# Second-layer single experts: fp32 matmuls straight from the weight slots in place of high and low parts

## The chip, the cores and the metric

The kernel runs on one core of a Trainium2 chip. The metric is the device time of one execution in microseconds; the profile is one execution taken apart by the hardware profiler. TensorE (PE in the profile, its weight loads PEld) multiplies, VectorE (DVE), ScalarE (ACT) and GpSimd (POOL) do the elementwise work, SyncE's queue (SP, SPq) issues nearly all weight transfers, and the core's 16 DMA engines carry them.

## The reference

Two layers over 256 latent and 256 context tokens of width 1024. The first has Fourier mixing and a short convolution, the second pooling and windowed attention; the change touches neither. After the mixer each layer has a mixture of 16 experts with top-2 routing. In the second layer only the 256 latent tokens pass through it:

```python
for e in range(N_EXPERTS):
    hid = jax.nn.silu(h @ w_gate[e]) * (h @ w_up[e])
    out = out + combine[:, e:e + 1] * (hid @ w_down[e])
```

An expert's gate and up are 1024 x 512 and its down is 512 x 1024, all fp32, 2 MB each: 6 MB an expert, 96 MB for the layer. All of it is read once from HBM.

## The kernel before

**Units.** The experts are ranked by load on the chip and dealt into units of 128 token slots: a single (`S`) has one expert for 128 slots, a pair (`P`) two experts with 64 each, a quad (`Q`) four with 32 each. For the second layer `PLAN[1] = "PPSPSPPQ"`, so eight units, numbered 0 to 7 here: pairs 0, 1, 3, 5, 6, singles 2 and 4, and the quad 7 at the end.

**A unit's work on TensorE.** `xpose1` makes the gathered tokens' transpose `xh`; `gu` does gate and up (8 steps over k each, into a 128 x 512 bank, by `mm_unit`, L933), `hidden` takes silu(gate) x up x weight, `hid_T` transposes that, `down1` does the 8 down matmuls (`mm_down`, L967), `combine1` brings the result back to token order (L1708) and adds it to H. In the loop (L1727 on) the order is: down of the unit before, up of this one, combine of the one before, transposes and gate of the next. A pair's or quad's experts use plain fp32 operands, in disjoint column groups of the array, side by side. A single's matmul is three products of fp32r parts (`mm3`, L517 to L519): high x high, high x low, low x high.

**Parts.** For a single, `Stream._prep` makes the parts of each weight load in two pieces: ScalarE writes the high part `whi` (L176), VectorE or, for each third piece, GpSimd the low part `wlo` (L180). The ring holds `NPIECE` = 4 pieces, which is two loads. The tokens and the hidden rows of singles are split as well (`split`, and `hl` in `hid_T`). Earlier stages of the kernel, the second layer's mixer last among them, use the same ring of parts.

**The stream of weights.** Every weight load is 1 MB and has a place in one list (`st.add`), in the order of use: for each unit its gate loads, then the down loads of the unit before, then its up loads. A pair has 4 loads for each matrix, a single 2, the quad 8. A load starts when a slot of 1 MB is free:

```python
def load(self):
    while self.free and self.loaded < min(len(self.src), self.limit):
        ...
        self.owner[i] = self.free.pop(0)
def _prep(self):
    ...
            if j == 1:
                self._release(i)
```

A slot of a pair or quad is free again when TensorE has read it (`done`), that of a single once both of its pieces are split (`_prep`, above), which comes right after its load in the program's order. All loads are issued by SP in one queue, so one that waits for its slot holds back those behind it. In the second layer there are 13 slots: 7 in the ring, one in `fp`, four in the phase's own pool (`EXTRA`), and one made of two 512 KB tiles (class `Two`: tiles `wa` and `wb`), which takes its load as two transfers (L140; a whole one is L147).

The order of instructions on each engine is set by the framework's planner, from the program's order and its own timeline.

Of the kernel before, what the change touches and what calls it, by code (L numbers as in the profile page):

```python
# [10 lines left out]
F32 = mybir.dt.float32  # L11
F32R = mybir.dt.float32r
# [6 lines left out]
KD = 8  # L19
# [9 lines left out]
RING, NPIECE = 7, 4  # L29
# [183 lines left out]
def backbone(ctx: ExitStack, tc: tile.TileContext, I, out):  # L213
    nc = tc.nc
    V, S, G, T, Q = nc.vector, nc.scalar, nc.gpsimd, nc.tensor, nc.sync

    cp = ctx.enter_context(tc.tile_pool(name="cp", bufs=1))
    ring = ctx.enter_context(tc.tile_pool(name="ring", bufs=1))
# [14 lines left out]
    def tr_t():  # L233
        return psum.tile([128, 512], F32, name="tr", tag="tr", bufs=2)


    st = Stream(tc, ring, RING, NPIECE)
# [59 lines left out]
    def expert(l, p):  # L297
        if p < FIXED[l]:
            return slice(p, p + 1)
        if (l, p) not in which:  # L300
            which[l, p] = nc.values_load(ids[l][0:1, p:p + 1], engines=[mybir.EngineType.SP], min_val=0,
                                         max_val=NE - 1)
        return ds(which[l, p], 1)

    def add_moe(l):
        def src(w, p, r0, c0):
            return [(lambda t: t, lambda: w[expert(l, p), r0:r0 + 512, c0:c0 + 512].rearrange(
                "a (k p) f -> (a p) k f", p=128))]

        def flat(t):  # L310
            return t.rearrange("p k f -> p (k f)")

        def rows_of(w, p, s):

            return [(flat, lambda: w[expert(l, p)].rearrange("a (p s j) f -> s (a p) (j f)", p=128, s=2)[s])]

        def put(name, w, u, pos, last=False):
            for s, (r0, c0) in enumerate(pos):
                for p in u:
                    st.add((name, l, p), src(w, p, r0, c0) if l == 0 or last else rows_of(w, p, s), len(u) == 1)  # L320

        wg, wu, wd = (I[n][l] for n in ("moe_w_gate", "moe_w_up", "moe_w_down"))
        rows2, cols2 = ((0, 0), (512, 0)), ((0, 0), (0, 512))
        for n, u in enumerate(UNITS[l]):
            put("g", wg, u, rows2)
            if n:
                put("d", wd, UNITS[l][n - 1], cols2)
            put("u", wu, u, rows2)
        put("d", wd, UNITS[l][-1], cols2, True)
# [186 lines left out]
    def mm3(o, lh, ll, rh, rl, first, last):  # L516
        T.matmul(o, lh, rh, start=first, stop=False)  # L517
        T.matmul(o, lh, rl, start=False, stop=False)  # L518
        T.matmul(o, ll, rh, start=False, stop=last)  # L519

    def split(hi, lo, x, eng):
        i = S.activation(hi, x, AF.Copy)  # L522
        eng.tensor_sub(lo, x, hi.bitcast(F32))  # L523
        return i
# [117 lines left out]
    with phase("even") as ep:  # L642
        def big(name, tag, dt=F32):
            return ep.tile([128, KD, 512], dt, name=name, tag=tag)
# [15 lines left out]
        xT = big("xT", "XT")  # L660
# [199 lines left out]
        r0 = []  # L860
# [20 lines left out]
        for half in range(2):  # L881
            banks = [mm_t() for _ in range(4)]
            hs = slice(half * 512, half * 512 + 512)
            for s in range(2):
                adas(4 + half * 2 + s)
                w = st.take(("eo", half))
# [33 lines left out]
    def mm_unit(o, l, n, name, xh, xl, s, first, last, between=()):  # L920

        u = UNITS[l][n]
        w = [st.take((name, l, p)) for p in u]
        i = st.taken - len(u)
        for k in range(4):
            kk = s * 4 + k
            if len(u) == 1:
                mm3(o, xh[:, kk], xl[:, kk], w[0].h(k), w[0].l(k), first and k == 0, last and k == 3)
            else:
                m = 128 // len(u)  # L930
                for h in range(len(u)):
                    hs = slice(h * m, h * m + m)
                    T.matmul(o[hs], xh[:, kk, hs].bitcast(F32), w[h][:, k], start=first and k == 0, stop=last and k == 3,  # L933
                             skip_group_check=True)
            if k == 1 and len(u) == 1:
                st.half()
            if k == 3:
                for h in range(len(u)):
                    st.done(i + h)
            if k % 2:  # L940
                for f in between[k // 2:k // 2 + 1]:
                    f()
# [11 lines left out]
    def mm_down(os, l, n, hh, hl, s):  # L954

        u = UNITS[l][n]
        w = [st.take(("d", l, p)) for p in u]
        i = st.taken - len(u)
        for k in range(4):
            j, o = 2 * s + k // 2, os[k % 2]  # L960
            if len(u) == 1:
                mm3(o, hh[:, j], hl[:, j], w[0].h(k), w[0].l(k), j == 0, j == 3)
            else:
                m = 128 // len(u)
                for h in range(len(u)):
                    hs = slice(h * m, h * m + m)
                    T.matmul(o[hs], hh[:, j, hs].bitcast(F32), w[h][:, k], start=j == 0, stop=j == 3,  # L967
                             skip_group_check=True)
            if k == 1 and len(u) == 1:
                st.half()  # L970
            if k == 3:
                for h in range(len(u)):
                    st.done(i + h)
# [82 lines left out]
    def hid_T(pool, hid, pair, rows=False):  # L1056
        pt = tr_t()
        for q in range(4):

            T.transpose(pt[:, q * 128:(q + 1) * 128], hid[:, q:512:4] if rows else hid[:, q * 128:(q + 1) * 128], idt)  # L1060
        hh = pool.tile([128, 4, 128], F32R, name="hh", tag="hh", bufs=1)
        if pair:
            V.tensor_copy(hh.bitcast(F32).rearrange("p k t -> p (k t)"), pt)
            return hh, None
        hl = pool.tile([128, 4, 128], F32R, name="hl", tag="hl", bufs=1)
        p4 = pt.rearrange("p (k t) -> p k t", k=4)
        S.activation(hh, p4, AF.Copy)  # L1067
        V.tensor_sub(hl, p4, hh.bitcast(F32))
        return hh, hl
# [64 lines left out]
    with phase("moe0") as mp:  # L1134
        xT = {}
# [26 lines left out]
        units = UNITS[0]  # L1162
# [126 lines left out]
        for n in range(NU):  # L1289
# [12 lines left out]
            hid = hidden(mp, pg, pu, slw[:, n:n + 1])  # L1302
# [26 lines left out]
        for c in range(2):  # L1329
            t = ("whi", "wlo")[c]  # L1330
# [19 lines left out]
    with phase("odd") as op:  # L1350
# [90 lines left out]
        w = st.take(("okv",), 256)  # L1441
# [15 lines left out]
        for b in range(2):  # L1457
            pt = tr_t()
# [6 lines left out]
        pt = tr_t()  # L1465
# [75 lines left out]
        units = [(b, c) for b in range(2) for c in range(4)]  # L1541
# [15 lines left out]
        fs = []  # L1557
# [16 lines left out]
        for n, u in enumerate(units):  # L1574
# [9 lines left out]
            if n == 4:  # L1584
                flush()
                rows(1, 3, 5, 1)
                t = op.tile([128, 2, D], F32, name="s4b", tag="band")
# [4 lines left out]
            if n in (4, 5):  # L1592
                w = st.take(("oo", n - 4))
# [26 lines left out]
    with phase("moe1") as mp:  # L1620
        for n in range(EXTRA):
            st.more(1, lambda n=n: mp.tile([128, 4, 512], F32, name="w", tag=f"w{n}"))
        st.load()
        m5b = mp.tile([128, D], F32, name="m5b1")
        spread(m5b, 1, 5, 0)
        units = UNITS[1]
        NU = len(units)
        ranks, ranksT = pm, None
        xT, slw, sgT, xg = {}, {}, {}, {}
# [38 lines left out]
        def xpose1(n, sg=None):  # L1668

            xh = mp.tile([128, KD, 128], F32R, name="xh1", tag="xh", bufs=2)  # L1670
            xl = mp.tile([128, KD, 128], F32R, name="xl1", tag="xl", bufs=1) if len(units[n]) == 1 else None
            for hf in range(2):
                pt = tr_t()
                for q in range(4):

                    ks = slice(hf * 4 + q, D, 8)
                    o = pt[:, q * 128:(q + 1) * 128]
                    if sg is None:
                        T.transpose(o, xg[n][:, ks], idt)
                    else:  # L1680
                        for c in range(2):
                            T.matmul(o, f1[c][:, ks], sg[:, c], start=(c == 0), stop=(c == 1))
                fs = slice(hf * 4, hf * 4 + 4)
                if xl is None:
                    (V.tensor_copy if hf else S.copy)(xh[:, fs].bitcast(F32).rearrange("p k t -> p (k t)"), pt)
                else:
                    split(xh[:, fs], xl[:, fs], pt.rearrange("p (k t) -> p k t", k=4), V)
            xT[n] = (xh, xl)

        def slotsT1(n):  # L1690
            pb, io = spread_ranks(units[n], ranksT, 256)
# [6 lines left out]
        def down1(n, hh, hl):  # L1698
            ys[n] = [x_t(f"{t}1", "Y", F32R) for t in ("yh", "yl")]
            down(mp, 1, n, hh, hl, *ys[n])  # L1700
# [25 lines left out]
        reg = any_over(mp, over)  # L1726
        for n in range(NU):  # L1727
            if n:
                down1(n - 1, *hid_T(mp, hid, len(units[n - 1]) > 1, True))
            pu = gu("u", 1, n, *xT[n])  # L1730
            hid = hidden(mp, pg, pu, slw[n])
            slotsT1(n)
            if n:
                combine1(n - 1)
            if n + 1 < NU:
                xpose1(n + 1)
                if n + 3 < NU:
                    slots1(n + 3)
                    gather1(n + 3)
                pg = gu("g", 1, n + 1, *xT[n + 1])  # L1740

        hh, hl = hid_T(mp, hid, len(units[-1]) > 1)
        gfb = mp.tile([128, D], F32, name="gfb", tag="xl", bufs=1)
        Q.dma_start(gfb, I["final_g"].partition_broadcast(128))
        yb = x_t("yb", "Y")
# [119 lines left out]
```

## Time and profile before

| | us |
|---|---|
| three runs | 1009.97 median, 1009.04 to 1010.44 |
| the profiled execution, its own time | 1012.91 |
| its span, first to last instruction | 1011.1 |
| granted clock, mean over the span | 0.958 of full speed |

The second layer's experts fill the last quarter. Their first matmul is at 751.5 us of the span; the phase's own loads begin at 737.9. In the stretches below, PEclk 1.00 is the 2.4 GHz level and 0.50 the 1.2 GHz one. A timeline row has start, length, engine, line, operation, tiles and the number of records merged; behind it in brackets the idle time before it and what ended it. A plain fp32 matmul leaves two records.

### The profile page before, as it was taken

The page shows a single profiled execution, that of the slowest core. Times are in us where ns is not written, and L with a number is a line of the kernel's source. Part 1 is how long each engine was busy: PE and PEld are TensorE (multiplying, and loading weights), DVE is VectorE, ACT ScalarE, POOL GpSimd, SP SyncE. Part 2 cuts the span into 40 slices and gives each one's busy share as a digit, 9 for nine tenths or more (in the row PEclk, how much of TensorE's full clock was granted, in tenths as well). Part 3 has the DMA queues.
Part 4 walks back from the last instruction along what each step waited for, and adds up shares of the span by engine and source line. Part 5 has one row for each costly group of instructions (what it writes and reads, how often), then busy time and mean ns, then how long its engine had stood idle before and what let it go on. Part 6 is the DMA issues. An engine that isn't in the chain of part 4 may idle for free. (4 is left out here: it accounts for less than half of the span.)

```text
span 1011.1 us, 12687 instructions
## 1 busy us (share of the span) xinstructions
PE 927.9 (92%) x4662; PEld 583.7 (58%) x4662; DVE 532.2 (53%) x921; ACT 340.3 (34%) x488; POOL 346.5 (34%) x239
## 2 busy tenths in 40 slices
PE   4999999978899999999999788999976999999973
PEld 2677677746675678558746567457553355544321
DVE  4552525286783777457935774547443265643212
ACT  4322113144563266246534362333211132411001
POOL 3350103335562746525823633023000143452112
PEclk9999999998899999999999989799977999999988
DMA  9973668948699799799699872296568799999993
GB/s 316 363 266 125 230 252 290 352 167 299 214 321 374 245 344 362 264 340 387 219 363 385 292 237 84 94 308 237 191 232 326 293 418 407 370 384 419 420 397 132
DMA packets 116276, 296.28 MB, mean 293 GB/s; under 512 B 6632, under 2 KB 16888, under 8 KB 105704
## 3 DMA queue, kind: packets, MB, share of 16 engines
q1 hardware_dynamic: 110184, 278.06, 75.0%
q0 software_dynamic: 5984, 17.26, 4.7%
q8 instruction: 40, 0.66, 0.3%
q14 instruction: 36, 0.29, 0.1%
q10 hardware_dynamic: 32, 0.01, 0.0%
HBM read 295.45 MB, written 4.24 MB: 296 GB/s over the span
## 5 line engine op out<-in xcount | busy, mean ns | idle before, releaser
L176 ACT ACTIVATE whi<-w 128x1024 fp32r<-128x1024 f32 x182 | 190.7, 1058 | 221.9 <-PE mm L519 87.0
L180 POOL TENSOR_TENSOR wlo<-w,whi 128x1024 fp32r<-128x1024 f32 x64 | 164.6, 2572 | 258.8 <-ACT whi L176 206.0
L180 DVE TENSOR_TENSOR wlo<-w,whi 128x1024 fp32r<-128x1024 f32 x118 | 181.1, 1546 | 92.5 <-ACT whi L176 91.8
L933 PE MATMUL mm<-w,xh 128*64 128x512 f32 (+1 forms) x616 | 150.9, 617 | 4.8 <-DMA w<-in_moe_w_up_dram 4.8
L528 POOL TENSOR_TENSOR H<-H,am 128x512 f32<-128x512 f32 x64 | 89.7, 1420 | 125.3 <-DVE am L527 122.9
L933 PEld LDWEIGHTS mm<-w,xh 128*64 128x64 f32 (+1 forms) x616 | 43.8, 135 | 88.4 <-issue 78.1
L517 PE MATMUL mm<-whi,xh 128*128 128x512 f32 x192 | 79.3, 413 | 1.9 <-DVE am L527 1.1
L518 PE MATMUL mm<-wlo,xh 128*128 128x512 f32 x192 | 78.6, 409 | 2.7 <-DVE wlo L180 2.3
L519 PE MATMUL mm<-whi,xl 128*128 128x512 f32 x192 | 78.1, 407 | 0.0
L527 DVE TENSOR_TENSOR am<-mm,m5b 128x512 f32<-128x512 f32 x64 | 42.9, 684 | 28.7 <-PE mm L1261 19.5
L1261 PE MATMUL mm<-y,seT 128*128 128x512 f32 x208 | 54.5, 397 | 0.2 <-ACT y L522 0.2
L517 PE MATMUL mm<-aTh,whi 128*128 128x512 f32 x128 | 52.4, 415 | 1.0 <-ACT aTh L678 1.0
L518 PE MATMUL mm<-aTl,whi 128*128 128x512 f32 x128 | 51.6, 403 | 1.1 <-POOL aTl L679 1.1
L519 PE MATMUL mm<-aTh,wlo 128*128 128x512 f32 x128 | 51.1, 400 | 0.0
L1261 PEld LDWEIGHTS mm<-y,seT 128*128 128x128 f32 x208 | 38.1, 188 | 15.5 <-issue 4.9
L518 PEld LDWEIGHTS mm<-wlo,xh 128*128 128x128 f32 x192 | 37.4, 195 | 14.4 <-DVE wlo L180 3.4
L517 PEld LDWEIGHTS mm<-whi,xh 128*128 128x128 f32 x192 | 37.5, 195 | 14.0 <-issue 4.2
L445 PE MATMUL yp<-w,sT 128*32 128x512 f32 x288 | 44.0, 624 | 0.0
L519 PEld LDWEIGHTS mm<-whi,xl 128*128 128x128 f32 x192 | 37.4, 195 | 7.7 <-DVE xl L523 0.3
L517 PE MATMUL yp<-whi,hh 128*128 128x512 f32 x96 | 38.2, 397 | 0.7 <-ACT hh L1067 0.7
L1053 DVE SCALAR_TENSOR_TENSOR sg<-sg,slw,mm 128x512 f32<-128x512 f32 x21 | 15.6, 742 | 43.9 <-PE mm L933 41.1
L518 PE MATMUL yp<-wlo,hh 128*128 128x512 f32 x96 | 38.4, 400 | 0.0
(363 smaller groups left out, 1545.2 us busy)
## 6 DMA issues: line engine op xcount, KB each, us to landing
w<-in_moe_w_gate_dram SPq DMA_DIRECT2D x60, 1024.0 KB, 11.3
w<-in_moe_w_down_dram SPq DMA_DIRECT2D x59, 1024.0 KB, 10.5
w<-in_moe_w_up_dram SPq DMA_DIRECT2D x57, 1024.0 KB, 9.7
w<-in_ada_w_dram SPq DMA_DIRECT2D x48, 1024.0 KB, 10.1
w<-in_even_w_in_dram SPq DMA_DIRECT2D x8, 1024.0 KB, 9.6
w<-in_odd_w_in_dram SPq DMA_DIRECT2D x5, 1024.0 KB, 14.3
w<-in_even_w_out_dram SPq DMA_DIRECT2D x4, 1024.0 KB, 7.9
s4b<-mrow SPq DMA_DIRECT2D x6, 512.0 KB
```

What stands on the lines that cost most here:

```text
L176: self.nc.scalar.activation(hi, t, AF.Copy)
L180: eng.tensor_sub(lo, t, hi.bitcast(F32))
L445: T.matmul(pa[32 * j:32 * j + 32, :], s_at(s * 4 + j, u), t[:, j, :], start=first and s == 0, stop=last and s == 1, skip_group_check=True)
L517: T.matmul(o, lh, rh, start=first, stop=False)
L518: T.matmul(o, lh, rl, start=False, stop=False)
L519: T.matmul(o, ll, rh, start=False, stop=last)
L527: V.tensor_mul(t, pp, m)
L528: eng.tensor_add(acc, acc, t)
L933: T.matmul(o[hs], xh[:, kk, hs].bitcast(F32), w[h][:, k], start=first and k == 0, stop=last and k == 3, skip_group_check=True)
L1053: V.scalar_tensor_tensor(sg, sg, w, pu, op0=OP.mult, op1=OP.mult)
L1261: marks["comb"] = T.matmul(pp, seT[n][:, c * 128:(c + 1) * 128], t[:, hs], start=(i == 0), stop=(i == 2 * len(ns) - 1))
```

## The change

The second layer's singles are no longer split. `put` marks none of that layer's loads as split, and `mm_unit` and `mm_down` choose the three products by whether a low part was passed instead of by the unit's size. `xpose1` copies the tokens without a low part, `hid_T` is called as for pairs. A single's matmuls thus run as plain fp32 over all 128 columns, on weights in their slots, and its slots are freed by TensorE. The memory of the ring's four high and four low pieces becomes four more slots, each a `Two` of one `whi` and one `wlo`, added behind the four `EXTRA` ones: 17 in all.

```diff
         def put(name, w, u, pos, last=False):
...
-                    st.add((name, l, p), src(w, p, r0, c0) if l == 0 or last else rows_of(w, p, s), len(u) == 1)
+                    st.add((name, l, p), src(w, p, r0, c0) if l == 0 or last else rows_of(w, p, s),
+                           l == 0 and len(u) == 1)
...
-            if len(u) == 1:
+            if xl is not None:
                 mm3(o, xh[:, kk], xl[:, kk], w[0].h(k), w[0].l(k), first and k == 0, last and k == 3)
...
-            if k == 1 and len(u) == 1:
+            if k == 1 and xl is not None:
                 st.half()
...
-            if len(u) == 1:
+            if hl is not None:
                 mm3(o, hh[:, j], hl[:, j], w[0].h(k), w[0].l(k), j == 0, j == 3)
...
         for n in range(EXTRA):
             st.more(1, lambda n=n: mp.tile([128, 4, 512], F32, name="w", tag=f"w{n}"))
+
+        for n in range(NPIECE):
+            st.more(1, lambda: Two(*(ring.tile([128, 1024], F32R, name="w2", tag=t, bufs=NPIECE).bitcast(F32)
+                                     for t in ("whi", "wlo"))))
         st.load()
...
-            xl = mp.tile([128, KD, 128], F32R, name="xl1", tag="xl", bufs=1) if len(units[n]) == 1 else None
...
-                if xl is None:
-                    (V.tensor_copy if hf else S.copy)(xh[:, fs].bitcast(F32).rearrange("p k t -> p (k t)"), pt)
-                else:
-                    split(xh[:, fs], xl[:, fs], pt.rearrange("p (k t) -> p k t", k=4), V)
-            xT[n] = (xh, xl)
+                (V.tensor_copy if hf else S.copy)(xh[:, fs].bitcast(F32).rearrange("p k t -> p (k t)"), pt)
+            xT[n] = (xh, None)
...
-                down1(n - 1, *hid_T(mp, hid, len(units[n - 1]) > 1, True))
+                down1(n - 1, *hid_T(mp, hid, True, True))
...
-        hh, hl = hid_T(mp, hid, len(units[-1]) > 1)
+        hh, hl = hid_T(mp, hid, True)
```

## Rows read from the trace of the kernel before

**Rows 1.** The page's first part: busy time and share of each engine.
```profile
PE 927.9 (92%) x4662; PEld 583.7 (58%) x4662; DVE 532.2 (53%) x921; ACT 340.3 (34%) x488; POOL 346.5 (34%) x239
```

**Rows 2.** Windows: busy us of each engine, then PEclk, DMA share, GB/s.
```profile
752.00:796.00 44.00, 35.79 (x157) 14.50 (x155) 15.18 (x53) 6.96 (x8) 5.52 (x4) 0.84 0.66 251
796.00:856.00 60.00, 57.70 (x262) 29.32 (x259) 30.08 (x46) 14.64 (x19) 19.12 (x13) 0.97 1.02 421
856.00:868.00 12.00, 10.67 (x50) 7.96 (x49) 9.93 (x15) 6.85 (x10) 5.61 (x4) 1.00 0.81 292
...
896.00:904.00 8.00, 8.00 (x31) 3.51 (x31) 1.17 (x2) 0.60 (x2) 3.01 (x2) 1.00 0.87 304
904.00:964.00 60.00, 59.84 (x311) 24.90 (x314) 17.11 (x26) 6.04 (x11) 13.40 (x11) 1.00 1.01 420
964.00:994.00 30.00, 19.53 (x90) 4.52 (x87) 3.50 (x5) 1.45 (x4) 4.03 (x4) 0.89 0.96 361
```

**Rows 3.** TensorE's timeline in the quad's up and down, 961 to 998 us.
```profile
961.19 3.91 PE L933 MATMUL mm<-w,xh 128*32 128x512 f32 x32
...
971.54 1.07 PE L933 MATMUL mm<-w,xh 128*32 128x512 f32 x3 [2.74 <-DMA w<-in_moe_w_up_dram]
...
978.89 0.66 PE L1060 MATMUL tr<-idt,sg 128*128 128x128 f32 x4 [0.84 <-DVE sg L1053]
...
980.33 1.06 PE L933 MATMUL yp<-w,hh 128*32 128x512 f32 x6 [0.78 <-DVE hh L1063]
...
988.36 1.04 PE L933 MATMUL yp<-w,hh 128*32 128x512 f32 x2 [2.17 <-SPq L1130]
...
989.34 1.98 PE L1763 MATMUL mm<-yb,sgT 128*128 128x512 f32 x4
...
993.63 3.62 PE L933 MATMUL yp<-w,hh 128*32 128x512 f32 x26 [1.33 <-SPq L1130]
```

**Rows 4.** SP's waits from 690 us on: total, times, longest.
```profile
SPq L147 <- PE mm L933: 62.4, 25, 14.4
SPq L147 <- DVE wlo L180: 56.5, 11, 11.9
```

**Rows 5.** SP's timeline: issues of weight loads in the second layer's experts.
```profile
737.94 2.14 SPq L147 DMA_DIRECT2D w<-in_moe_w_gate_dram  x4
...
755.17 6.63 SPq L147 DMA_DIRECT2D w<-in_moe_w_down_dram  x3
...
768.19 15.46 SPq L147 DMA_DIRECT2D w<-in_moe_w_gate_dram  x2
793.14 2.05 SPq L147 DMA_DIRECT2D w<-in_moe_w_down_dram  x4
...
956.56 25.02 SPq L147 DMA_DIRECT2D w<-in_moe_w_down_dram  x8
```

**Rows 6.** TensorE's timeline: pairs' gates, a single's first and last product, two waits.
```profile
783.31 11.10 PE L933 MATMUL mm<-w,xh 128*64 128x512 f32 x42
...
811.13 0.47 PE L517 MATMUL mm<-whi,xh 128*128 128x512 f32 x1
...
816.54 0.40 PE L519 MATMUL mm<-whi,xl 128*128 128x512 f32 x1
...
820.43 0.80 PE L518 MATMUL mm<-wlo,xh 128*128 128x512 f32 x1 [2.29 <-DVE wlo L180]
...
863.76 0.47 PE L517 MATMUL mm<-whi,xh 128*128 128x512 f32 x1 [1.11 <-DVE am L527]
...
888.25 7.09 PE L933 MATMUL mm<-w,xh 128*64 128x512 f32 x32
```

**Rows 7.** A window of 4 us behind the first of those waits.
```profile
820.00:824.00 4.00, 3.56 (x8) 2.12 (x10) 3.27 (x5) 2.12 (x2) 0.00 (x0) 0.57 1.04 429
```

**Rows 8.** DMA issues from 740 us on: the token gathers, median us to landing.
```profile
xg<-fd,sli POOLq DMA_INDIRECT x7, 7.2
```

**Rows 9.** SP's timeline: the first half of a load into the slot of two tiles.
```profile
802.85 0.34 SPq L140 DMA_DIRECT2D wa<-in_moe_w_up_dram  x1
```

More of the change, by code (lines that the diff above doesn't have):

```diff
@@ L968, in mm_down @@
                              skip_group_check=True)
-            if k == 1 and len(u) == 1:
+            if k == 1 and hl is not None:
                 st.half()
```

## The prediction

> **What bounds the kernel now.** I read the page first. TensorE is busy for 92% of the span [rows 1], which speaks against a change that gives it more to do. An average over stages doesn't settle that, so the second layer's experts come next, in windows [rows 2]. From 752 to 796 us the DMA engines move 251 GB/s, from 796 to 856 they are full at 421, twice they fall back (292 and 304), and from 904 on they are full again. TensorE is busy all the while, with under 3 us idle from 796 to 856 and next to none from 904 to 964. Only in the last stretch, 964 to 994, is it idle for a third of the time, with the DMA engines still loaded. The timeline there [rows 3] names the wait: the quad's up waits 2.74 us for a load of up weights, the second half of its down 2.17 and 1.33 us for loads (SPq stands there for a DMA that came last). The last load lands at about 993.6, and the last down matmul ends at 993.63 + 3.62 = 997.25; from there to the end of the span are 13.9 us which the change doesn't touch.
>
> So the end is set by the last weight load. TensorE outruns the transfers from 796 on, lives on what is stored in the slots, and finds them empty at 964. What would bring the last load forward is transfer time not used earlier. Measured against 421 GB/s, 752 to 796 loses 44 x (1 - 251/421) = 17.8 us, 856 to 868 loses 12 x (1 - 292/421) = 3.7, 896 to 904 loses 8 x (1 - 304/421) = 2.2: together 23.7 us. SP's waits say why [rows 4]: 62.4 us for slots that TensorE still reads, 56.5 us for slots whose low part isn't made. The first case of the second kind is in SP's timeline [rows 5]. The two gate loads of unit 2, the first single, take from 768.19 to 783.65, and the next issue is at 793.14: in the program's order the second goes into the slot that the first one's split frees, and unit 1's down load into the slot that the second one's frees. SP can't pass them.
>
> **The change, part by part.**
>
> *Products.* A single has 16 gate and up steps and 8 down steps; two singles make 48. Now a step is three products: from the first to the last of 24 in a gate are 816.54 - 811.13 = 5.41 us, 0.235 each, 0.706 a step [rows 6]. After it is one plain fp32 matmul of 128 columns, two records. The pair's gate gives the spacing: 32 records in two column groups in 7.09 us, (7.09 - 0.59)/15 = 0.433 a record, 0.866 a matmul. That shape at full width stands once in the trace, four records in 1.98 us [rows 3], the first one's start and the last one's tail included, so 0.99 is an upper bound. I take 0.866, since the singles' matmuls come in rows of eight as the pair's do: 48 x (0.866 - 0.706) = 7.7 us more, at most 13.6.
>
> The Trainium skill speaks against the change here: its page FP8 and Floating Point Precision, section TensorE Precision Notes, has true fp32 as four passes through the array. If one product is one pass, a step costs 4 x 0.235 = 0.94 us and the sum is 11.2 us instead of 7.7; the trace's two records in 0.866 us lie between three and four of its own products.
>
> *Splits.* Gone are 24 pieces on ScalarE, 16 on VectorE and 8 on GpSimd, and the two halves of the tokens' and hidden rows' splits. None of these engines sets the end, so they count only where TensorE waited: 2.29 us for a low part at 820.43 and 1.11 us for a bank that VectorE was late to read at 863.76 [rows 6]. Behind the first the granted clock over 4 us is 0.57 of full [rows 7]; the eight records there stand at 0.235/0.57 = 0.41 us and cost 1.4 us more. Together 4.8 us less. TensorE's net is +2.9 us, with 0 and +13.6 as bounds (0 if the planner's new order closes some of the small gaps between the blocks too).
>
> *Slots.* The list's order for the first units is gate 0, up 0, gate 1, down 0, up 1, gate 2, down 1, up 2, gate 3. Thirteen slots hold it to the first load of down 0. After, the four new slots take all of down 0, and their memory is free when the mixer's last product has read the parts, ahead of the routing and so of these loads. With gate and up 0 read by 768 [rows 5], the old kernel has issued 21 loads and the chained 22nd goes at 783.65; the new one has issued 25. One load is 1.049 MB, 2.49 us at 421 GB/s. From 739.7 on the new kernel has 16 loads (gate 1, down 0 and the eight after them), half a MB of the modulation row and two gathers of half a MB: about 17.5 x 2.49 = 43.6 us, to 783.3. Then all is full until TensorE is half through gate 1 and gives back two slots, as now: 42 records from 783.31 take 11.10 us [rows 6], the 16th ends near 788; first bytes flow at 789. That leaves 5.5 us idle of the 17.8, so 12.3 us are won by 796. The two later losses, behind splits of the singles' loads too, are worth 5.9 us more. The last load lands 12.3 to 18.2 us earlier, at 981.3 to 975.4.
>
> At the end 17 slots hold the quad's eight up and eight down loads together. Now the eight down issues stretch over 25.02 us [rows 5], since they wait for up slots; after, they follow the release of unit 6's down slots, which lies ahead of the quad's up at 961.19 [rows 3].
>
> *What a single's slot now costs.* It is free only after TensorE's use instead of after the split, so of the four new slots two make good for the four pieces, which held two loads. It shows where TensorE is at a single: 6.9 us for two slots, in which 2.8 loads arrive. I take 1 to 3 us of idle transfers there, within the two ends above.
>
> *DMA work moved.* The final gain's row waited for the low part of the tokens and can now go early: 512 KB, 1.2 us, in a stretch with idle time. Gathers of tokens on GpSimd's queue land in 7.2 us [rows 8], mostly beside full weight queues, so the new backlog at 773 isn't priced higher.
>
> *Halves.* A `Two` slot is loaded by two transfers of 512 KB. The four new ones take 4 x 96/17, some 22 loads. The cost on SP is a second issue of 0.34 us [rows 9], 7.5 us over 230 us, hidden since SP mostly waits for slots [rows 4]. The first such load in the stretch, at 802.85, fell into the window of 421 GB/s [rows 2], so I take no loss of rate.
>
> **The sum.** TensorE comes to the quad's up at 961.2 + 2.9 = 964.1. Its 16 steps take 16 x 0.433 = 6.9, to 971.0; from there to the first down matmul are now 2.3 us (978.89 - 0.84 = 978.05 to 980.33), so 973.3; first half of down 3.5; second half 3.5 plus the combine's four records, 2.0 [rows 3]: 982.3, against 997.25 now. That is 15.0 us earlier if no load is waited for. The second half's loads are needed at 976.8. By the better transfer figure (975.4) they are there; by the poorer one (981.3) they end the work 12.3 us earlier. I take the middle, 13.6. The profiled execution's own 1012.91 becomes 999.3, its span 997.5. That execution lies 2.9 us above the median of the three runs, so the forecast is 1009.97 - 13.6 = 996.4.
>
> **Rivals.**
>
> *The lead is two slots only.* If the singles' slots, held longer, eat what the missing split chain gives, what remains is a lead of two loads, 5.0 us: 1005.0. For it: SP's larger wait is for TensorE's reads, not for low parts [rows 4]. Against: the chain from 768 to 793 is gone whatever the later slots do.
>
> *The last load comes when it did.* The 292 and 304 GB/s windows move elsewhere and the early lead is used up by full slots: 1010, same. Against it: from 904 to 964 transfers ran at 420 GB/s without a gap, so an early lead has nowhere to go but to the end.
>
> *Slower: half transfers cost transfer time.* The two windows of poor rate hold the issues of halves as well. If not SP's wait but the halves cost those 3.7 + 2.2 us, that is 0.85 us for each of the seven such loads now, and 22 more would cost 18.7. The windows would stay too, so the lead is 12.3: the last load lands 6.4 us later, 1016.4. It decides from 12.3/22 = 0.6 us a load. Against it: the full windows hold halves as well, at 420.
>
> The Trainium skill's page DMA: Bandwidth & Descriptors asks for transfers of 1 MiB or more (Rules for kernel authors) and has a fixed 2 us for each (Anatomy of one DMA, for GpSimd's path). If these didn't overlap, an estimate of 22 x 2 = 44 us would be lost; no window here shows such a loss.
>
> **Chances.** Forecast with its own range 993 to 1001: 0.60. Two slots only, 1001 to 1008: 0.19. Last load as before, 1008 to 1012: 0.08. Slower: 0.07. Faster than 993, by more small gaps closed on TensorE: 0.06. The range 992.5 to 1005 takes the forecast, most of the second case and a little of the last. A measurement of this kernel can tell 0.2%, about 2 us, from no change. Faster by more: 0.60 + 0.19 + 0.06 = 0.85; within: 0.08; slower: 0.07.
>
> **What would show it.** Right: no splits behind 740 us; SP's issues without a pause from 768 to 788; windows from 752 to 796 near 370 GB/s and no dips at the singles; singles' records 0.43 us apart; the quad's up without a wait. Wrong: fp32 records of singles further apart than 0.43, windows below 400 GB/s where halves fly, gathers landing later than 9 us, or the quad still waiting for loads at 965 to 993 as now.

## The result, and the profile after

The changed kernel takes 1002.19 us (median of four runs, 999.87 to 1004.19) against 1010.21 for the kernel before on the same chip: ratio 0.989, 95% interval 0.9848 to 0.9932. Two more sets gave 0.9878 (0.9839 to 0.9916) and 0.9897 (0.985 to 0.9944). The forecast of 996.4 is a ratio of 0.9866, inside all three intervals; the median lies 5.8 us above it, inside the range.

The profiled execution took 999.87 us, its span is 998.1, against 1011.1. Of these 13.0 us not all are the change's: the code ahead of the experts is the same but for the loads of down 0 issued there, yet their first gate starts at 748.32 and stood at 751.49 before, and that start differs as much between executions of one kernel (last section). So times below count from the first gate (**g0**). From there to the end of the span it is 249.8 us after and 259.6 before: 9.8 us less in the stage that was changed.

TensorE's timeline after: the first gate, the wait for gathered tokens, the down of unit 0, steps of the second single (unit 4) and the down of unit 3 behind them, and the tail. The columns are those of [rows 3]; line numbers have moved by one.

```profile
748.32 7.94 PE L934 MATMUL mm<-w,xh 128*64 128x512 f32 x32
...
777.21 1.94 PE L1683 MATMUL tr<-idt,xg 128*128 128x128 f32 x8 [5.70 <-DMA xg<-fd,sli]
...
797.41 7.09 PE L968 MATMUL yp<-w,hh 128*64 128x512 f32 x32
...
858.36 10.55 PE L934 MATMUL mm<-w,xh 128*128 128x512 f32 x24
...
873.04 7.09 PE L968 MATMUL yp<-w,hh 128*64 128x512 f32 x32
...
955.08 3.20 PE L934 MATMUL mm<-w,xh 128*32 128x512 f32 x27
...
963.58 0.66 PE L1061 MATMUL tr<-idt,sg 128*128 128x128 f32 x4 [0.84 <-DVE sg L1054]
965.02 1.05 PE L934 MATMUL yp<-w,hh 128*32 128x512 f32 x4 [0.78 <-DVE hh L1064]
967.24 1.04 PE L934 MATMUL yp<-w,hh 128*32 128x512 f32 x2 [1.17 <-DMA w<-in_moe_w_down_dram]
969.94 5.32 PE L934 MATMUL yp<-w,hh 128*32 128x512 f32 x28 [1.66 <-SPq L1131]
...
980.87 3.62 PE L934 MATMUL yp<-w,hh 128*32 128x512 f32 x26 [1.53 <-SPq L1131]
```

The quad's up, at 955.08, waits for nothing now; its down still waits three times for loads (1.17, 1.66 and 1.53 us), and the last 26 records begin when the last load has landed, as at 993.63 in [rows 3]. That landing is 232.6 us behind g0, 242.1 before: 9.6 less. A single's 24 records take 10.55 us, (10.55 - 0.59)/23 = 0.433 each.

The windows show where the 9.6 us come from. First before, in windows that [rows 2] didn't have, then after, each window 3.2 us earlier, so that both stand alike to g0; columns as in [rows 2].

```profile
724.00:738.00 14.00, 10.68 (x69) 8.18 (x65) 6.88 (x12) 4.26 (x8) 0.57 (x1) 0.89 0.07 30
738.00:752.00 14.00, 10.33 (x48) 9.83 (x50) 5.67 (x38) 0.59 (x1) 0.56 (x1) 0.62 0.93 355
...
796.00:808.00 12.00, 12.00 (x57) 3.71 (x54) 1.35 (x3) 0.60 (x1) 0.00 (x0) 1.00 1.01 427
808.00:872.00 64.00, 60.38 (x272) 36.75 (x273) 41.12 (x62) 24.23 (x30) 28.56 (x20) 0.97 0.98 396
872.00:884.00 12.00, 12.00 (x54) 6.00 (x53) 5.85 (x5) 3.42 (x5) 2.24 (x1) 1.00 1.02 413
884.00:960.00 76.00, 75.42 (x370) 32.17 (x369) 23.73 (x41) 9.73 (x16) 22.59 (x15) 1.00 1.00 408
```

```profile
720.80:734.80 14.00, 10.69 (x66) 8.17 (x63) 6.88 (x12) 4.25 (x8) 0.57 (x1) 0.88 0.74 278
734.80:748.80 14.00, 10.30 (x47) 9.81 (x49) 5.67 (x38) 0.58 (x1) 0.56 (x1) 0.63 0.98 377
748.80:792.80 44.00, 35.84 (x157) 14.59 (x155) 10.41 (x50) 3.06 (x4) 3.15 (x3) 0.84 0.76 294
792.80:804.80 12.00, 12.00 (x57) 3.91 (x54) 1.60 (x3) 0.82 (x2) 0.00 (x0) 1.00 0.84 303
804.80:868.80 64.00, 64.00 (x242) 29.85 (x241) 21.93 (x49) 5.71 (x10) 18.08 (x15) 1.00 1.02 411
868.80:880.80 12.00, 12.00 (x52) 4.87 (x51) 2.52 (x4) 1.79 (x3) 0.00 (x0) 1.00 0.65 241
880.80:956.80 76.00, 76.00 (x374) 32.09 (x377) 22.59 (x41) 7.22 (x14) 18.39 (x15) 1.00 1.02 416
```

A window's gain in transfer time is its length times the difference of the rates over 421. From the top: 14 x (278 - 30)/421 = +8.2 us, +0.7, then 44 x (294 - 251)/421 = +4.5 (251 from [rows 2]): a lead of 13.4. Then -3.5, +2.3, -4.9 and +1.4: 4.7 of it are given back. The sum, 8.7, is the 9.6 of the landing within 0.9. TensorE is busy without a gap from 793 to 957, and the two bad windows lie in that stretch.

SP's timeline after says what it issued, and its waits in two stretches (786 to 812, 858 to 884) what held it in the bad windows.

```profile
724.04 4.55 SPq L140 DMA_DIRECT2D w<-in_moe_w_down_dram  x8
...
734.76 1.81 SPq L147 DMA_DIRECT2D w<-in_moe_w_gate_dram  x4
...
761.31 23.97 SPq L147 DMA_DIRECT2D w<-in_moe_w_down_dram  x4
...
799.37 3.77 SPq L140 DMA_DIRECT2D w<-in_moe_w_gate_dram  x5
...
868.93 11.55 SPq L147 DMA_DIRECT2D w<-in_moe_w_gate_dram  x4
```

```profile
SPq L140 <- PE yp L968: 8.7, 3, 6.1
SPq L147 <- PE mm L934: 5.2, 2, 3.9
...
SPq L147 <- PE mm L934: 12.6, 2, 6.3
SPq L147 <- PE yp L968: 9.6, 2, 7.3
```

The eight halves of down 0 go into the new slots at 724.04, 14 us ahead of the phase's first loads before [rows 5], and ahead of gate 1 (734.76), which the list has in front of them. By 776 all slots are full: the last of the four loads at 761.31 can't go before 785.28, while TensorE waits 5.70 us for gathered tokens. The slots of down 0 are read only at 797.41, and SP, which has to refill them next (799.37), waits 8.7 us for it, in three waits. In the second stretch it waits 6.3 us at a time for the gate and up of unit 4, which TensorE works through from 858.36 on, and then 7.3 us for slots of the down of unit 3, which comes only behind them, at 873.04. Both times the list has the down loads ahead of the next up, while TensorE, in the planner's order, does that up first. With SP held, little flies, in windows of 4 us:

```profile
772.00:776.00 4.00, 0.00 (x0) 0.00 (x0) 0.02 (x1) 0.00 (x0) 0.12 (x1) 0.50 0.94 379
776.00:780.00 4.00, 2.79 (x14) 2.58 (x16) 0.69 (x1) 0.58 (x1) 0.00 (x0) 0.50 0.09 34
780.00:784.00 4.00, 4.00 (x14) 1.29 (x16) 1.36 (x8) 0.00 (x0) 1.00 (x1) 0.66 0.25 66
784.00:788.00 4.00, 4.00 (x22) 1.41 (x19) 0.00 (x0) 0.00 (x0) 0.00 (x0) 1.00 0.59 174
...
796.00:800.00 4.00, 4.00 (x20) 1.13 (x19) 1.14 (x2) 0.00 (x0) 0.00 (x0) 1.00 0.78 324
800.00:804.00 4.00, 4.00 (x22) 1.29 (x18) 0.00 (x0) 0.29 (x1) 0.00 (x0) 1.00 0.71 196
804.00:808.00 4.00, 4.00 (x27) 3.23 (x24) 3.21 (x7) 1.49 (x3) 0.76 (x1) 1.00 0.96 282
...
872.00:876.00 4.00, 4.00 (x17) 1.24 (x17) 1.14 (x2) 0.00 (x0) 0.00 (x0) 1.00 0.42 170
876.00:880.00 4.00, 4.00 (x20) 1.15 (x16) 0.05 (x1) 0.60 (x1) 0.00 (x0) 1.00 0.55 158
```

### The profile page after: what moved, and what is told of

Its sections match the earlier page's. It is cut to its first block, busy times and chain, and to the rows that moved or that the text cites. A ratio compares the mean times of both kernels' runs of the same rounds, so it can differ in the third digit from the quotient of the medians.

```text
span 998.1 us, 12560 instructions
## 1 busy us (share of the span) xinstructions
PE 923.3 (93%) x4614; PEld 571.9 (57%) x4614; DVE 502.6 (50%) x903; ACT 313.5 (31%) x460; POOL 323.6 (32%) x231
## 5 line engine op out<-in xcount | busy, mean ns | idle before, releaser
L176 ACT ACTIVATE whi<-w 128x1024 fp32r<-128x1024 f32 x162 | 169.8, 1058 | 182.2 <-PE mm L520 78.2
L180 POOL TENSOR_TENSOR wlo<-w,whi 128x1024 fp32r<-128x1024 f32 x57 | 145.9, 2561 | 228.2 <-ACT whi L176 190.1
L180 DVE TENSOR_TENSOR wlo<-w,whi 128x1024 fp32r<-128x1024 f32 x105 | 156.1, 1498 | 78.6 <-ACT whi L176 78.1
L934 PE MATMUL mm<-w,xh 128*64 128x512 f32 (+2 forms) x680 | 172.9, 602 | 0.5 <-DMA w<-in_moe_w_up_dram 0.5
L934 PEld LDWEIGHTS mm<-w,xh 128*64 128x64 f32 (+2 forms) x680 | 54.2, 138 | 94.4 <-issue 89.1
L518 PE MATMUL mm<-whi,xh 128*128 128x512 f32 x160 | 66.1, 413 | 0.8 <-ACT xh L523 0.8
L519 PE MATMUL mm<-wlo,xh 128*128 128x512 f32 x160 | 65.2, 408 | 0.3 <-POOL wlo L180 0.3
L520 PE MATMUL mm<-whi,xl 128*128 128x512 f32 x160 | 64.9, 406 | 0.0
L528 DVE TENSOR_TENSOR am<-mm,m5b 128x512 f32<-128x512 f32 x64 | 42.9, 685 | 28.2 <-PE mm L1262 19.5
L968 PE MATMUL yp<-w,hh 128*64 128x512 f32 (+1 forms) x176 | 42.8, 595 | 0.0
L1053 ACT ACTIVATE sg<-mm 128x512 f32<-128x512 f32 x21 | 12.4, 589 | 85.3 <-PE mm L934 79.8
L934 PE MATMUL yp<-w,hh 128*64 128x512 f32 (+1 forms) x160 | 33.7, 643 | 5.1 <-SPq L1131 3.2
## 6 DMA issues: line engine op xcount, KB each, us to landing
w<-in_moe_w_gate_dram SPq DMA_DIRECT2D x54, 1024.0 KB, 11.5
```

Source lines behind the costliest of these rows:

```text
L176: self.nc.scalar.activation(hi, t, AF.Copy)
L180: eng.tensor_sub(lo, t, hi.bitcast(F32))
L528: V.tensor_mul(t, pp, m)
```

## The experiments

**Theory:** the last load sets the end, and it comes earlier by what the four slots let the queue run ahead, less what it loses where all 17 slots are full and TensorE hasn't read the next one. **Rivals:** the freed split chain gives the gain, slots or not; TensorE's own work sets the end; half transfers cost transfer time.

The table has, for each profiled execution, from the rows of TensorE's timeline, the time from g0 to the last 26 records (the last load's landing) and to the end of the span, beside the runs.

| kernel | g0 to last load, us | g0 to end, us | median, us | ratio to before (95%) |
|---|---|---|---|---|
| before | 242.1 | 259.6 | 1010.21 | |
| changed | 232.6 | 249.8 | 1002.19 | 0.989 (0.9848 to 0.9932) |
| after_again | 233.0 | 250.2 | 1001.25 | 0.9878 (0.9839 to 0.9916) |
| changed_third | 234.7 | 251.8 | 1001.15 | 0.9897 (0.985 to 0.9944) |
| no_slots | 241.1 | 257.8 | 1008.2 | 0.9961 (0.9936 to 0.9986) |
| two_slots | 238.3 | 255.7 | 1007.09 | 0.9956 (0.9924 to 0.9987) |
| all_halves | 234.7 | 251.8 | 1002.09 | 0.9892 (0.9861 to 0.9923) |
| extra_products | 233.0 | 250.1 | 1001.68 | 0.9914 (0.988 to 0.9948) |
| late_single | 231.8 | 250.8 | 999.55 | 0.9856 (0.9817 to 0.9895) |
| singles_late | 230.9 | 248.0 | 1000.56 | 0.9883 (0.9851 to 0.9915) |
| no_gather_wait | 230.6 | 247.7 | 999.25 | 0.9879 (0.9849 to 0.9909) |
| both_late1 | 227.7 | 244.7 | 997.33 | 0.985 (0.9815 to 0.9885) |
| both_late2 | 228.6 | 245.9 | 994.15 | 0.9831 (0.9797 to 0.9865) |
| both_late2_again | 228.6 | 245.6 | 996.56 | 0.9864 (0.9822 to 0.9906) |

### The slots alone

The changed kernel as it is (twice, beside others), without its new slots, and with two of the four.

```diff
-        for n in range(NPIECE):                     # no_slots: these three lines are gone
-            st.more(1, lambda: Two(...))
+        for n in range(2):                          # two_slots: two of the four
+            st.more(1, lambda: Two(...))
```

> The changed kernel itself, as the measure for the others of this group. From its first runs: ratio to before 0.987 to 0.993, some 1000 to 1004 us. Its profile should again show idle transfers at three places: about 776 to 786 us (all slots full, TensorE waiting for the first gather), 796 to 808 and 872 to 880 us (SP waiting for slots that TensorE reads).

> The changed kernel as it is, beside the next one on the same chip. All theories: 0.988 of before, about 1000 to 1003 us; first gate of the experts to the last load's landing 232.5 to 233.5 us.

> The change without the four new slots: singles in plain fp32, 13 slots. Theory 1 (the gain is the lead that the slots give to the transfers): the lead is gone and the singles hold their slots longer, so the last load lands no earlier than before or later; 1008 to 1018 us. Theory 2 (the gain is that SP is no longer stuck behind the splits; the slots matter little): 1000 to 1005 us. Theory 3 (TensorE's own time decides, the products and the lost waits): 1000 to 1004 us, like the changed kernel.

> The change with two of the four new slots, 15 in all. Theory 1: half of the lead, so half way between the kernel without the new slots and the changed one; 1004 to 1011 us, idle transfers at the singles longer than in the changed kernel. Theories 2 and 3: as the changed kernel, 1000 to 1004 us.

Without the slots the last load lands 1.1 us earlier than before, with two 3.9, with four 7.5 to 9.6 (the three executions of the changed kernel, which differ by 2.1 us; the other kernels have one profile each). So most of the gain is made by the slots: in the runs of this set 7.0 of 11.5 us (1012.79 before, 1008.2 without the slots, 1001.25 with four), and the rest of the change alone is worth 0.4% (0.14 to 0.64). The steps at the last load, 2.8 and then 3.6 to 5.7 us, lie below the 5.0 us that two loads take at 421 GB/s, or about there. In the runs two slots can't be told from none, where half of the way was expected.

Without the slots, windows that stand to g0 (744.99) as those above show what the missing splits do:

```profile
745.50:789.50 44.00, 36.02 (x157) 14.66 (x155) 10.38 (x50) 3.06 (x4) 3.15 (x3) 0.84 0.73 278
...
801.50:865.50 64.00, 64.00 (x244) 30.32 (x245) 23.20 (x51) 6.52 (x11) 18.06 (x15) 1.00 1.01 413
865.50:877.50 12.00, 12.00 (x46) 4.28 (x45) 1.19 (x2) 0.78 (x2) 0.00 (x0) 1.00 0.68 243
```

Against before, the first wins 44 x (278 - 251)/421 = 2.8 us of transfers, the second 64 x (413 - 396)/421 = 2.6, and the third loses 12 x (413 - 243)/421 = 4.8. What the missing splits give is nearly all lost again at the second single. Now 794 to 806 us, first without the slots, then with two.

```profile
794.00:806.00 12.00, 12.00 (x63) 6.05 (x60) 5.38 (x12) 1.78 (x3) 1.69 (x2) 1.00 1.01 413
```

```profile
794.00:806.00 12.00, 12.00 (x61) 5.10 (x57) 3.60 (x6) 1.78 (x3) 0.00 (x0) 1.00 0.65 243
```

Without new slots there is no bad window here; with two there is one, as with four. It comes with the slots: part of the lead that they give is lost in it. The later one, 868 to 882 us, is there in all three (242 GB/s without the slots, 218 with two), so it doesn't need the new slots. Before, that stretch stood at 413 GB/s; the singles' slots, which TensorE now frees, are the likely cause, and singles_late below bears that out.

### TensorE's time, and the halves

extra_products has eight more fp32 matmuls of a single's shape in unit 6, on operands that are in memory anyway; their result isn't used. all_halves loads 55 more weight loads as two transfers each.

```diff
             hid = hidden(mp, pg, pu, slw[n])
+            if n == 6:
+                spare = tr_t()
+                for k in range(KD):
+                    T.matmul(spare, xT[n][0][:, k].bitcast(F32), m5b[:, 0:512], start=(k == 0), stop=(k == KD - 1))
```

```diff
+                elif len(src.shape) == 2 and len(dst(t).shape) == 2 and src.shape[-1] == 2048:
+                    for j in range(2):
+                        self.nc.sync.dma_start(dst(t)[:, 1024 * j:1024 * j + 1024], src[:, 1024 * j:1024 * j + 1024])
                 elif i in self.behind:
```

> The changed kernel with eight more plain fp32 products of 128 x 512 (6.9 us at 0.866 us each) in the last pair, on operands that lie in SBUF, into a bank that nobody reads. They stand for a higher price of TensorE's work. Theory 1 (the last load sets the end, TensorE has some 10 us of slack by then): 0 to +2.5 us, so 1000 to 1005 us. Theory 3 (TensorE's time is the end, as it is busy without a gap from 797 to 957 us): +6 to +7 us, so 1006 to 1010 us.

> The changed kernel with nearly every weight load of the second layer's experts issued as two transfers of half the columns (512 KB), as the slots of two tiles are. If a half costs transfer time, as the slower rival has it from 0.85 us a load, some 60 more of them cost 40 us or more. If it costs only a second issue of 0.34 us on SP, which mostly waits: 1000 to 1004 us, as the changed kernel.

The tail with the extra products, on TensorE:

```profile
963.82 3.20 PE L934 MATMUL mm<-w,xh 128*32 128x512 f32 x26
...
973.17 4.48 PE L934 MATMUL yp<-w,hh 128*32 128x512 f32 x34 [0.78 <-DVE hh L1064]
...
981.88 3.62 PE L934 MATMUL yp<-w,hh 128*32 128x512 f32 x26 [1.28 <-SPq L1131]
```

The last part of the quad's up starts 215.0 us behind g0 (748.86) instead of 206.8, 8.2 later. The two earlier waits of the down are gone, the last load lands 0.5 us later at most, and the end is where it was (250.1 us against 249.8 and 250.2). TensorE had that much time to spare; the rival that its products set the end falls for work this late. For work ahead of 880 us, where SP waits for TensorE's reads, it is not tested: the singles' steps take 0.16 us longer than before, 7.7 us in all, and no kernel here varies that price (singles_late below moves these steps behind 895 us).

The 55 more halves put the last load 1.7 to 2.1 us behind two of the changed kernel's executions and level with the third: at most 2.1/55 = 0.04 us a load, where the slower rival needed 0.6. The run medians agree (1002.09 against 1001.15 to 1002.19). That rival falls.

### Where the lead is lost

Singles late (two orders of the units), and the wait for unit 1's gathered tokens taken away: the tokens of unit 1 are transposed with those of unit 0, by the path without a gather.

```diff
-PLAN = ("SSSPSSSPSSSPS", "PPSPSPPQ")
+PLAN = ("SSSPSSSPSSSPS", "PPSPPPSQ")                # late_single, both_late1
+PLAN = ("SSSPSSSPSSSPS", "PPPPPSSQ")                # singles_late, both_late2; FIXED (2, 4)
```

```diff
-        for n in (1, 2):                            # no_gather_wait, both_late1, both_late2
-            slots1(n)
-            gather1(n)
+        xpose1(1, slots1(1))
+        slots1(2)
+        gather1(2)
...
-                xpose1(n + 1)
+                if n:
+                    xpose1(n + 1)
```

> The changed kernel with its second single moved behind the pairs, next to the quad (plan PPSPPPSQ). If the end is set by the idle time of transfers, and the dip of 872 to 880 us comes from slots that are full while TensorE takes a single, the dip goes, since the slots are no longer full so late: the last load lands up to 5 us earlier, 996 to 1001 us. If that dip has no part in the end, because TensorE is busy without a gap from 797 to 957 us anyway: the same as the changed kernel, within 1.5 us.

> The changed kernel with both singles behind the five pairs (plan PPPPPSSQ; only four experts are fixed ahead of the routing, so that unit 2 is a pair). Theory 1, idle transfers at full slots set the end: the dips at 800 to 808 and 872 to 880 us (3.5 and 4.9 us of transfer time in the changed kernel's profile) shrink; 994 to 1000 us, last load some 3 to 8 us earlier from the first gate on. Theory 3, TensorE's own time sets the end: no change, 1000 to 1004 us.

> The changed kernel, but unit 1's tokens are picked and transposed by matmul from the rows in SBUF, as unit 0's are, so that TensorE doesn't wait 5.7 us for a gather at 771 to 777 us with all slots full. The idle transfers of 776 to 786 us come from that wait if theory 1 holds: TensorE starts unit 1's gate some 5 to 8 us earlier, gives slots back earlier, and the last load lands 4 to 8 us earlier; 993 to 999 us. If that idle time is not on the path: the 3 to 6 us of added matmuls replace the wait, 1000 to 1004 us.

> Two of the earlier edits together: unit 1's tokens by matmul (no gather wait) and the second single behind the pairs (plan PPSPPPSQ). By theory 1 the transfers' idle time adds up: the last load landed 230.6 us behind the first gate without the gather wait and 231.8 with the late single, against 232.6 and 233.0 in the changed kernel; together some 229 to 230, and 995 to 999 us. If idle time at full slots only moves from one place to another, nothing adds: 230.5 to 231.5, 998 to 1001 us.

> The same with both singles behind the five pairs (plan PPPPPSSQ, four fixed experts). Added up from 230.6 and 230.9: some 228.5 to 229.5 us from the first gate to the last landing, 994 to 998 us. If idle time only moves: 230 to 231 us, 997 to 1000 us; the routing's result is needed 8 loads earlier here, so that SP may wait for it near 756 us.

> The kernel without the wait for gathered tokens and with both singles as units 5 and 6, beside the changed kernel on the same chip. If what the changed kernel loses to full slots is what is won back: 4 to 5 us below the changed kernel (0.983 of before, 995 to 998 us), and the last load lands 4 to 5 us sooner behind the first gate (228 to 229 us). If the earlier 994.15 us was the spread between runs (rival): within 2 us of the changed kernel.

With late_single, where unit 4 is a pair, the window of 170 GB/s is gone, and a smaller dip stands ahead of it, where TensorE reads the down of the first single (850.35 to 857.5 us):

```profile
852.00:856.00 4.00, 4.00 (x10) 1.71 (x9) 0.00 (x0) 0.00 (x0) 0.00 (x0) 1.00 0.91 337
856.00:860.00 4.00, 4.00 (x23) 2.99 (x21) 2.54 (x4) 1.67 (x3) 0.00 (x0) 1.00 0.85 254
...
872.00:876.00 4.00, 4.00 (x22) 1.29 (x18) 0.97 (x2) 1.19 (x2) 0.00 (x0) 1.00 1.01 422
```

The last load lands only 0.8 us sooner than in the earliest execution of the changed kernel. The end of late_single didn't follow: its last 26 records took 5.32 us instead of 3.62, in a window (980 to 986 us) at a granted clock of 0.72.

With singles_late units 0 to 4 are all pairs. In windows that stand to g0 (751.22) as the two bad ones above:

```profile
795.70:807.70 12.00, 12.00 (x56) 3.82 (x53) 1.51 (x3) 0.73 (x2) 0.00 (x0) 1.00 0.68 244
...
871.70:883.70 12.00, 12.00 (x54) 4.76 (x51) 3.22 (x11) 1.78 (x3) 0.74 (x1) 1.00 1.02 422
```

The later dip is gone (422 GB/s in place of 241), while the first has grown (244 in place of 303). So the later one comes with the single, and the first needs none. The last load lands 1.7 us sooner, again against the earliest; part of what is won at one dip is lost at the other.

Without the gather wait the same stretch of 4 us windows reads:

```profile
772.00:776.00 4.00, 4.00 (x19) 4.00 (x18) 0.00 (x0) 0.59 (x1) 0.00 (x0) 0.87 0.93 381
776.00:780.00 4.00, 4.00 (x23) 2.27 (x24) 1.86 (x9) 0.00 (x0) 1.12 (x1) 1.00 0.03 10
```

TensorE no longer stands still for 5.70 us and its clock is back at 1.00 by 776. With 7.88 us of added matmuls in place of the wait, unit 1's gate starts 28.2 us behind g0 instead of 31.6, and the last load lands 2.0 us sooner than in the earliest execution of the changed kernel.

Each of the three edits gives less at the last load (0.8, 1.7 and 2.0 us) than was expected (up to 5, 3 to 8, 4 to 8), and none more than the 2.1 us by which executions of the changed kernel differ. In the runs none alone can be told from it.

Both together win 4.0 us and more at the last load (227.7 and 228.6, against 232.6 to 234.7), and on the same chip 996.56 us against 1001.15 for the changed kernel; the earlier set gave 994.15. The intervals against before overlap, and so do the six runs of each on that chip (995.38 to 1002.00 and 996.35 to 1006.58), but all three medians and all three profiles point the same way. Which of the two orders is better isn't shown: both_late1 has the earliest landing, both_late2 the lowest median.

## Why the prediction was right, and where it was off

*What bounds the kernel:* right in the main. That the last load sets the end, in spite of TensorE's 92% [rows 1], is tested after the change (extra_products) and only read from [rows 3] before it. But ahead of 880 us SP waits for TensorE's reads, and for longer than the forecast allowed (5.5 us by 796, 1 to 3 us at the singles).

*Products:* right. Records of a single are 0.433 us apart, 0.866 a step, as taken from the pair's gate. The row agrees with that and not with the 0.94 us estimated from one product for each of the Trainium skill's four passes (FP8 and Floating Point Precision, TensorE Precision Notes). It doesn't speak against four passes of 0.22 us.

*TensorE's net:* off by more than its bounds. It reaches the quad's up 206.8 us behind g0 against 209.7 [rows 3], 2.9 us sooner instead of 2.9 later. In the windows above, from 752 and from 748.8 on, its idle time fell by 4.2 us, of which the forecast had counted two waits, 3.4 us; where the other 5 us come from isn't taken apart. It didn't change the time, since TensorE then waits for the down's loads.

*Slots, the early lead:* right in size, 13.4 us against 12.3, but by luck. Of the 13.4 only 4.5 fall into the 44 us for which the 12.3 were worked out. The other 8.9 lie ahead: the loads of down 0 left at 724, ahead of the routing's end, where the forecast let the new backlog start at 739.7. The slots were then full from 776 on, not from 783, and 776 to 788 lost 9.4 us of transfers (34, 66 and 174 GB/s) in place of 5.5. At the end, too, the quad's eight down issues still stretch over 22.54 us from 946.59 on, 25.02 before [rows 5], where the forecast had them go ahead of the quad's up.

*The later windows:* this is the step that failed, by size. "What a single's slot now costs" was put at 1 to 3 us of idle transfers, and the last load 12.3 to 18.2 us earlier. In windows of 4 us the dip at 796 to 808 (324, 196 and 282 GB/s) is worth 4.4 us of transfers at 420 GB/s, that at 872 to 880 (170 and 158) 4.9. They replace the 5.9 us of dips before [rows 2]. So the lead after 793 didn't grow by up to 5.9, but lost 4.7; the last load came 9.6 us sooner, and the stage is 9.8 us shorter (9.4 and 7.8 in the other two executions) in place of 13.6. Only the second dip comes with a single (singles_late). The first most likely hangs on down 0, which fills the new slots from 724 and is read at 797.41: the windows with none and two slots fit that, but a kernel that puts other loads there wasn't tried.

*The rivals.* Two slots only: the measured 1002.19 is 2.8 us from this rival's 1005.0 and 5.8 from the forecast's 996.4. It lies in the rival's part of the chances (1001 to 1008), not in the forecast's own (993 to 1001), and inside the range because that takes in most of the rival's part. Half of its mechanism holds: without the new slots, what the missing splits give is nearly all lost again (1.1 us at the last load). The other half doesn't: the four slots are then worth 6.4 to 8.5 us, more than two loads. The last load as before: wrong as a whole, but its mechanism, a lead used up by full slots, takes a third of the lead. The argument against it looked at 904 to 964 us only, and the loss lies ahead of that. Halves: excluded above; in and just ahead of the two poor windows of [rows 2] SP waited for low parts (10.7 and 5.3 us at the longest).

*What would show it:* no splits behind 740, singles' records at 0.43 and the quad's up without a wait came true. No pause of SP at 768 to 788, 370 GB/s from 752 to 796 (294 in the 44 us from 748.8 on) and no dips at the singles did not. Of the signs of being wrong two came: the quad's down still waits for loads, and halves fly in windows below 400 GB/s, though all_halves shows that they aren't the cause.

## What to carry to other kernels

When two engines look full, ask which one's earlier idle time can't be made up: here the transfers ran full from 881 to 957 us anyway (416 GB/s, 408 before), so what was lost ahead of that wasn't made up, and 8 us of TensorE's work late in the stage cost at most 0.5 us. More slots in a queue with a fixed order give a lead only until all are full; from there TensorE's reads pace the queue, so a load that is fetched early and read late (down 0, fetched 73 us ahead) and a wait on TensorE that holds a slot are the places to look for lost transfers. Taking one away can move the loss to another: three edits gave 0.8 to 2.0 us each, and two together 4.0 and more. Compare profiled executions from the start of the changed stage, since the part ahead varied by 8 us here.

## What was unexpected of the hardware

- The experts' first gate came between 744.99 and 752.78 us in the profiled executions, in two of one and the same kernel (both_late2) at 746.54 and 749.60; the kernel before ran from 1005.27 to 1020.05 us over all sets, much wider than its first three runs.
- Near the end of the changed kernel the DMA engines are fully loaded and yet slower than the 420 GB/s of [rows 2]: 387 GB/s at a share of 1.04. The cause is open.

```profile
956.00:976.00 20.00, 14.81 (x96) 4.20 (x88) 3.27 (x5) 0.00 (x0) 3.44 (x3) 0.91 1.04 387
```

- Gathers of tokens landed in a median of 8.2 us, 7.2 before [rows 8], with the weight queue fuller beside them (one execution each).
